# Attention's value product in plain float32, other buffer and hold-back counts, and attention traced at high priority, in a hybrid decoder layer

## Chip, cores and metric

The kernel runs on one core of a Trainium2 chip. The metric is the device time of one execution in microseconds, as the median of several runs. All arrays are float32 in the chip's main memory (DRAM).

## What is computed

One decoder layer over 2048 tokens of width 1024. An RMS norm and one input projection feed three groups of heads: differential softmax attention (4 heads, 128 wide), a gated linear recurrence (HGRN2) and a gated DeltaNet. Their outputs are concatenated, projected and added to the residual; then come a norm, a gated MLP of width 2816 with a causal convolution of width 3, and a final norm. The change touches attention:

```python
s = jnp.einsum("bhmqd,bhmkd->bhmqk", qi, kt).astype(jnp.float32) * scale
s = jnp.where(kpos[None, :] <= qpos[:, None], s, MASK_NEG)
p = jax.nn.softmax(s, axis=-1)
pd = p[:, :, 0] - lam * p[:, :, 1]
return jnp.einsum("bhqk,bhkv->bhqv", pd.astype(vt.dtype), vt)
...
o = rmsnorm(o, subln_w) * (1.0 - lambda_init)
```

and the place of the MLP's down projection in the order of the work:

```python
h = h + jnp.einsum("btf,fd->btd", jax.nn.silu(gate) * val, ffn_w_down[l])
```

## The kernel before

Large products are made of three products of type float32r: each operand is split into a high and a low part (`split`, L86), and `mm3` (L94 to L98) adds high by high, high by low and low by high. L88 (ScalarE) writes the high part and L89 (VectorE) the low one. TensorE's products of 128 rows by 512 columns on L96 to L98 are nearly all of its work; "three-term product" below means one of them. There are 9528 in the program, before and after.

Attention (`attention`, L871) goes head by head and, in a head, by blocks of 128 queries from the last block to the first. A block's keys come in chunks of 512. For each chunk and each of the two softmax maps `att_probs` makes two score products and, in the diagonal chunk, a mask product (L917, L920), a negated row maximum on VectorE (L921) and the exponential on ScalarE (L923); the two maps are then joined into one matrix on ScalarE and VectorE (L942, L943). `att_pv`, called one block later, turns each chunk over with four TensorE transposes (L954), splits it into `ph` and `pl` (L957), and multiplies both with the values, which stand in memory already split in two halves of 128 columns (L962, 256 columns each). At the block's end the two halves of the result are added (L965, L967), normed (L969 to L972), turned over (L973) and stored in `s_mix` (L976).

The keys 0 to 1023 are worked on during the input projection, with pools of their own (`XB`). Blocks 8 to 15 come later, among the MLP of the first 1024 tokens: `ffn_block` (up projection), then `down`, whose steps of 24 three-term products each load a weight tile and a tile of `s_g` (L1264 to L1270). `Pump` (L62) sets how far the attention's generator has been advanced at each MLP step; it is due by `PUMP1`. At the step (3, 8) of `down` the loop stops, attention is finished, and the output projection of tokens 1024 to 2047 runs (`residual`, L1054, called at L1027) with one `down` step drawn in after every second of its eight token tiles (L1030). `forms` (L1116) then prepares that half's operands for `up7` (L1151), a product scheme with seven products in place of eight, and a second `down` ends the kernel.

The text of the program does not set the order on an engine. The Tile framework's scheduler places the instructions on each of the five engines by readiness and by a priority that follows the order in which they were traced. Each engine then works through its own list in order.

Of the kernel before, what the change touches and what calls it, by code (L numbers as in the profile page):

```python
# [9 lines left out]
F32 = mybir.dt.float32  # L10
# [9 lines left out]
P = 128  # L20
# [6 lines left out]
EPS = 1e-6  # L27

P0_BUFS = 8
P1_BUFS = 4  # L30
S_BUFS = 2
T_BUFS = 1
XB = 6, 4, 2, 1, 2
NORM_PD = 2

# [6 lines left out]
AP_LEAD = 1  # L42

PUMP0 = 0
PUMP1 = 66
OFF = dict(aq=0, ak=512, av=1024, hq=1536, hf=1792, hi=2048, hg=2304,
           dq=2560, dk=2816, dv=3072, dz=3328, ab=3584)

# [31 lines left out]
class K:  # L80
# [66 lines left out]
    def scratch(self, ctx):  # L147
        d = ctx.enter_context(self.tc.tile_pool(name="scratch", bufs=1, space=DRAM))
        self.s_q = d.tile([4, P, 2, 2, T], F32R, name="s_q")
        self.s_k = d.tile([4, P, 2, T], F32R, name="s_k")  # L150
        self.s_v = d.tile([4, T, 2, P], F32R, name="s_v")
        self.s_dn = d.tile([8, P, T], F32, name="s_dn")
        self.s_hg = d.tile([8, P, T], F32, name="s_hg")
        self.s_mix = d.tile([8, P, T], F32, name="s_mix")
        self.s_h = d.tile([T, D], F32, name="s_h")
        self.s_g = d.tile([NF, P, T], F32, name="s_g")
# [152 lines left out]
    def proj_block(self, hf, t2, u, halo, kind, c0, i, w):  # L309
# [23 lines left out]
        if kind == "av":  # L333
            nc.scalar.copy(o, pt)
            pv = self.pp.tile([P, 512], F32, name="pp")
            for j in range(4):
                nc.tensor.transpose(pv[:, j * P:(j + 1) * P], o[:, j * P:(j + 1) * P], self.ident)
            eh, el = et("eh", F32R), et("el", F32R)
            self.split(eh, el, pv)
            for j, e in enumerate((eh, el)):  # L340
                nc.sync.dma_start(self.s_v[i, gs, j].bitcast(F32).rearrange("(k p) v -> p k v", p=P),
                                  e.bitcast(F32).rearrange("p (k v) -> p k v", v=P))
            return
        if kind == "hi":
            nc.scalar.copy(o, pt)
# [513 lines left out]

    def att_open(self, ctx, p0_bufs, p1_bufs, s_bufs, t_bufs, slots, side="left"):  # L860
        pool = partial(self.tc.tile_pool, side=side, reuse_waits="tile")
        self.p_bufs, self.kslots = (p0_bufs, p1_bufs), slots
        self.kq = ctx.enter_context(pool(name="kq", bufs=1))
        self.ap = ctx.enter_context(pool(name="ap", bufs=2))
        self.sm = ctx.enter_context(pool(name="sm", bufs=2))
        self.pss = ctx.enter_context(pool(name="pss", bufs=s_bufs, space=PSUM))
        self.pst = ctx.enter_context(pool(name="pst", bufs=t_bufs, space=PSUM))
        pso = ctx.enter_context(pool(name="pso", bufs=1, space=PSUM))
        self.oc = pso.tile([P, 2, 256], F32, name="o")

    def attention(self, b0, b1):  # L871

        nc, kq = self.nc, self.kq
        nkc = -(-b1 // 4)
        last = None
        for h in range(4):
            kS, vS = [None] * nkc, [None] * nkc
            for kc in reversed(range(nkc)):
                ts = slice(kc * 512, (kc + 1) * 512)
                slot = (h * nkc + kc) % self.kslots  # L880
                kS[kc] = kq.tile([P, 2, 512], F32R, name=f"k{slot}")
                nc.gpsimd.dma_start(kS[kc], self.s_k[h, :, :, ts])
                vS[kc] = kq.tile([P, 4, 2, P], F32R, name=f"v{slot}")
                nc.gpsimd.dma_start(vS[kc].rearrange("p k i v -> p k (i v)"),
                                    self.s_v[h, ts].rearrange("(k p) i v -> p k (i v)", p=P))
            for b in reversed(range(b0, b1)):
                if b % 2 == 1 or b == b1 - 1:
                    qS = self.ap.tile([P, 2, 2, 256], F32R, name="q")
                    q0 = b // 2 * 256
                    nc.gpsimd.dma_start(qS.rearrange("p m i q -> p (m i) q"),  # L890
                                        self.s_q[h, :, :, :, q0:q0 + 256].rearrange("p m i q -> p (m i) q"))
                pd = self.att_probs(kS, qS, b)
                if last:
                    self.att_pv(*last)
                last = h, b, pd, vS
                yield b + 1
        self.att_pv(*last)
# [47 lines left out]

    def att_pv(self, h, b, pd, vS):
        nc, sm = self.nc, self.sm
        oc = self.oc[:, b % 2]
        for c, pc in enumerate(pd):
            n = pc.shape[1]  # L950
            pt = self.pst.tile([P, 512], F32, name="t")
            for k in range(n // P):
                ks = slice(k * P, (k + 1) * P)
                nc.tensor.transpose(pt[:, ks], pc[:, ks], self.ident)  # L954
            ph = self.ap.tile([P, 512], F32R, name="ph")
            pl = self.ap.tile([P, 512], F32R, name="pl")
            self.split(ph[:, 0:n], pl[:, 0:n], pt[:, 0:n])  # L957
            for k in range(n // P):
                ks = slice(k * P, (k + 1) * P)
                vt = vS[c][:, k].rearrange("p i v -> p (i v)")  # L960
                for i, x in enumerate((ph, pl)):
                    nc.tensor.matmul(oc[:, 0:256], lhsT=x[:, ks], rhs=vt, start=c == 0 and k == 0 and i == 0,  # L962
                                     stop=c == len(pd) - 1 and ks.stop == n and i == 1)
        ol = sm.tile([P, P], F32, name="ol")
        nc.scalar.copy(ol, oc[:, P:2 * P])  # L965
        on = sm.tile([P, P], F32, name="on")
        nc.vector.tensor_tensor(on, oc[:, 0:P], ol, op=ALU.add)  # L967
        ss = sm.tile([P, 1], F32, name="ss")
        nc.scalar.activation(ol, on, AF.Square, accum_out=ss)  # L969
        rs = sm.tile([P, 1], F32, name="rs")  # L970
        self.rsqrt(rs, ss, 1.0 / P, EPS)
        nc.vector.tensor_scalar(on, on, rs, None, op0=ALU.mult)  # L972
        nc.tensor.transpose(oc[:, 0:P], on, self.ident)  # L973
        mx = sm.tile([P, P], F32, name="mx")
        nc.scalar.activation(mx, oc[:, 0:P], AF.Copy, scale=self.subln)
        nc.sync.dma_start(self.s_mix[h, :, b * P:(b + 1) * P], mx)  # L976


    def tail(self, cd, out):
# [5 lines left out]
        with ExitStack() as ctx:  # L985
# [5 lines left out]
            with ExitStack() as c1:  # L991
# [7 lines left out]
                                      lambda s, g, cs, pv: self.hi_lo(u[s][0][g][:, :, cs], u[s][1][g][:, :, cs], pv)))  # L999
                cd.close()  # L1000
                self.st = pool(c1, "cs", bufs=2)
                self.att_open(ca, P0_BUFS, P1_BUFS, S_BUFS, T_BUFS, 4, side="right")
                att = Pump(self.attention(8, 16), 4 * 100)
                pump = lambda n: att.upto((n - PUMP0) / (PUMP1 - PUMP0))
                for f in range(NF):
# [2 lines left out]
            with ExitStack() as c1:  # L1008
                self.st = pool(c1, "ds", bufs=2)
                down = self.down([0, 1], out, 1, main)  # L1010
                for s, dc, f in down:
                    n = 2 * s + dc
                    if (n, f) == (3, 8):
                        break
                    pump(2 * NF + n * NF // 2 + f // 2)
                    if (n, f) == (1, NF):
# [10 lines left out]
                for n, _ in enumerate(self.residual([2, 3], range(4), self.s_h, put, ws)):  # L1027
                    if n == 4:
                        B = next(forms)
                    if n % 2:  # L1030
                        next(down)
                for _ in chain(forms, down):
                    pass
# [329 lines left out]
```

## Time and profile before

| | |
|---|---|
| median of 3 runs | 3026.0 us (3024.95 to 3026.33) |
| the profiled execution | 3026.32 us |
| its span | 3024.6 us |
| TensorE busy (PE) | 2866.8 us, 95% |
| VectorE busy (DVE) | 1987.2 us, 66% |
| ScalarE busy (ACT) | 1393.7 us, 46% |
| GpSimd busy (POOL) | 373.5 us, 12% |
| mean granted TensorE clock | 0.975 |

Busy time is the time in which an engine has at least one instruction under way. A TensorE product's own length covers more than its share of the engine, because products overlap: the distance between the starts of two neighbours is what one of them costs. The clock is granted at 2.4 GHz or at half of that, 1.2 GHz.

### The profile page before, as it was taken

How to read it: one execution, taken by the hardware profiler on the slowest of the kernel's cores; microseconds unless marked ns; L12 is line 12 of the kernel's file. 1: busy time of each engine (PE TensorE's matmuls, PEld its weight loads, DVE VectorE, ACT ScalarE, POOL GpSimd, SP SyncE). 2: the span in 40 equal slices, each digit the busy share in tenths (PEclk: the TensorE clock that was granted, in tenths of full speed). 3: DMA queues.
4: the chain of work that ended last, by engine and by line, in shares of the span. 5: the costliest groups of instructions: out<-in, count | busy, mean ns of one | idle time of the engine just before them, and what ended most of it. 6: DMA issues, size and time to landing. Idle time of an engine off the chain costs nothing.

```text
span 3024.6 us, 50228 instructions
## 1 busy us (share of the span) xinstructions
PE 2866.8 (95%) x19746; PEld 2331.8 (77%) x19746; DVE 1987.2 (66%) x3535; ACT 1393.7 (46%) x2536; POOL 373.5 (12%) x567
## 2 busy tenths in 40 slices
PE   8899999999998899999999999999777999999998
PEld 6688877788776678887888888887555788888886
DVE  4144887578584766755677766767637788777454
ACT  3234456423222244443566666566634444444443
POOL 1001221111000102101111100001001222220000
PEclk9999999999998899999999999999888999999999
DMA  8565355243744643213423455854034222224674
GB/s 231 132 159 159 101 145 145 77 120 96 179 109 124 198 155 96 70 60 99 115 62 97 132 162 172 270 172 123 13 120 163 88 77 83 77 78 141 221 257 154
DMA packets 382928, 395.58 MB, mean 131 GB/s; under 512 B 68635, under 2 KB 280163, under 8 KB 382691
## 3 DMA queue, kind: packets, MB, share of 16 engines
q1 hardware_dynamic: 343395, 346.22, 37.4%
q0 software_dynamic: 39296, 46.14, 6.1%
q8 instruction: 155, 2.54, 0.4%
q14 instruction: 82, 0.67, 0.1%
HBM read 285.34 MB, written 106.95 MB: 130 GB/s over the span
## 4 chain that ended last, share of the span: by engine, by line
PE 87%; DVE 5%; DMA 3%; ACT 3%; issue 1%; POOL 0%; SPq 0%; POOLq 0%; ACTq 0%; DVEq 0%
PE pp L96 17%; PE pp L97 17%; PE pp L98 17%; PE pd L96 6%; PE pd L97 6%; PE pd L98 6%; PE o L962 4%; PE s L917 4%; PE t L954 2%; PE t L438 1%; PE t L804 1%; ACT p L923 1%; DMA x<-in_x_dram 1%; DMA h<-s_h 1%; DMA two<-s_mix 1%
## 5 line engine op out<-in xcount | busy, mean ns | idle before, releaser
L96 PE MATMUL pp<-uh,wh 128*128 128x512 f32 x896 | 360.6, 403 | 0.1
L97 PE MATMUL pp<-ul,wh 128*128 128x512 f32 x896 | 357.8, 399 | 0.3 <-DVE ul L191 0.3
L98 PE MATMUL pp<-uh,wl 128*128 128x512 f32 x896 | 357.1, 399 | 0.0
L89 DVE TENSOR_TENSOR wl<-two,wh 128x1024 fp32r<-128x1024 f32 x176 | 210.8, 1223 | 171.7 <-ACT wh L88 171.1
L1214 DVE SCALAR_TENSOR_TENSOR cv<-raw,columns,cv 128x512 f32<-128x512 f32 (+1 forms) x264 | 244.3, 925 | 70.3 <-ACT cv L1211 67.2
L96 PE MATMUL pd<-wh 128*128 128x512 f32 x704 | 257.8, 396 | 11.1 <-ACT wh L88 11.1
L88 ACT CAST wh<-two 128x1024 fp32r<-128x1024 f32 x176 | 178.7, 1052 | 184.4 <-PE pd L97 129.5
L921 DVE TENSOR_REDUCE nb<-s 128x1 f32<-128x512 f32 (+3 forms) x320 | 193.1, 608 | 107.2 <-PE s L920 65.0
L97 PE MATMUL pd<-wl,wh 128*128 128x512 f32 x704 | 258.3, 396 | 4.9 <-DVE wl L89 4.9
L923 ACT ACTIVATE p<-s,nb 128x512 f32<-128x512 f32 (+3 forms) x320 | 199.9, 626 | 122.2 <-DVE nb L921 105.4
L98 PE MATMUL pd<-wh,wl 128*128 128x512 f32 x704 | 248.3, 393 | 0.0
L96 PE MATMUL pp<-f,wh 128*128 128x512 f32 x616 | 241.3, 397 | 7.1 <-ACT wh L88 7.1
L97 PE MATMUL pp<-f,wh 128*128 128x512 f32 x616 | 244.5, 397 | 0.0
L98 PE MATMUL pp<-f,wl 128*128 128x512 f32 x616 | 237.1, 396 | 0.0
L917 PE MATMUL s<-k,q 128*128 128x512 f32 (+3 forms) x640 | 191.8, 390 | 25.4 <-ACT p L923 25.0
L98 PEld LDWEIGHTS pp<-uh,wl 128*128 128x128 f32 x896 | 170.2, 190 | 35.2 <-issue 0.2
L97 PEld LDWEIGHTS pp<-ul,wh 128*128 128x128 f32 x896 | 170.4, 190 | 34.5 <-DVE ul L191 1.0
L96 PEld LDWEIGHTS pp<-uh,wh 128*128 128x128 f32 x896 | 170.5, 190 | 34.1 <-ACT uh L190 0.5
L104 POOL TENSOR_TENSOR rs<-rs,mhalf 128x1 f32<-128x1 f32 x112 | 69.4, 623 | 1019.5 <-DVE rs L103 824.5
L96 PEld LDWEIGHTS pd<-wh 128*128 128x128 f32 x704 | 133.7, 190 | 40.8 <-ACT wh L88 13.2
L97 PEld LDWEIGHTS pd<-wl,wh 128*128 128x128 f32 x704 | 134.3, 191 | 33.4 <-DVE wl L89 5.4
L98 PEld LDWEIGHTS pd<-wh,wl 128*128 128x128 f32 x704 | 133.2, 189 | 28.0 <-DVE wl L89 0.2
(324 smaller groups left out, 6358.4 us busy)
## 6 DMA issues: line engine op xcount, KB each, us to landing
wu<-in_ffn_w_up_dram SPq DMA_DIRECT2D x88, 512.0 KB, 3.8
two<-in_ffn_w_down_dram SPq DMA_DIRECT2D x88, 512.0 KB, 3.8
two<-s_g SPq DMA_DIRECT2D x88, 512.0 KB, 4.7
wr<-in_w_in_dram SPq DMA_DIRECT2D x56, 512.0 KB, 4.8
q<-s_q POOLq DMA_DIRECT2D x32, 512.0 KB, 5.6
s_h<-h SPq DMA_DIRECT2D x32, 512.0 KB, 3.2
v<-s_v POOLq DMA_DIRECT2D x28, 512.0 KB, 5.4
k<-s_k POOLq DMA_DIRECT2D x28, 512.0 KB, 5.7
```

The costliest lines, as they stand in the source:

```text
L88: self.nc.scalar.copy(hi, src)
L89: self.nc.vector.tensor_tensor(lo, src, hi.bitcast(F32), op=ALU.subtract)
L96: mm(ps, lhsT=a[0], rhs=b[0], start=start, stop=False)
L97: mm(ps, lhsT=a[0], rhs=b[1], start=False, stop=False)
L98: mm(ps, lhsT=a[1], rhs=b[0], start=False, stop=stop)
L104: nc.gpsimd.tensor_tensor(out, out, self.mhalf[:, 0:1].broadcast_to(list(out.shape)), op=ALU.pow)
L917: nc.tensor.matmul(ps[:, 0:n], lhsT=qS[:, m, i, qs], rhs=kS[c][:, m, 0:n], start=i == 0, stop=i == 1 and not diag)
L921: nc.vector.tensor_reduce(nb[:, c, m:m + 1], ps[:, 0:n], axis=AX.X, op=ALU.max, negate=True)
L923: nc.scalar.activation(t, ps[:, 0:n], AF.Exp, bias=nb[:, c, m:m + 1], accum_out=ls[:, c, m:m + 1])
L954: nc.tensor.transpose(pt[:, ks], pc[:, ks], self.ident)
L962: nc.tensor.matmul(oc[:, 0:256], lhsT=x[:, ks], rhs=vt, start=c == 0 and k == 0 and i == 0, stop=c == len(pd) - 1 and ks.stop == n and i == 1)
L1214: nc.vector.scalar_tensor_tensor(c, r[e][:, j:j + n], self.fcw_l[j][:, idx:idx + 1], c, op0=mult, op1=ALU.add)
```

## The change

The probabilities and the values stay plain float32 in attention's second product: no split of the values when they are projected (L338), none of the probabilities (L957), one product of 128 columns per tile of 128 keys in place of two of 256, and no addition of halves. The block's last transpose gets a place of its own in the accumulator bank. Score buffers of the second map grow from 4 to 7, the slots for keys and values from 4 to 5 with another rule for their turn. Both halves of attention's work in a block are traced inside `high_priority()`. `PUMP1` goes from 66 to 62. The `down` loop stops at (2, 14), not (3, 8), and 13 steps, not 4, are drawn in among the eight token tiles of `residual`.

```diff
-P1_BUFS = 4
+P1_BUFS = 7
+K_SLOTS = 5
-PUMP1 = 66
+PUMP1 = 62
+HELD = 2, 14
-        self.s_v = d.tile([4, T, 2, P], F32R, name="s_v")
+        self.s_v = d.tile([4, T, P], F32, name="s_v")
-            eh, el = et("eh", F32R), et("el", F32R)
-            self.split(eh, el, pv)
-            for j, e in enumerate((eh, el)):
-                nc.sync.dma_start(self.s_v[i, gs, j].bitcast(F32).rearrange("(k p) v -> p k v", p=P),
-                                  e.bitcast(F32).rearrange("p (k v) -> p k v", v=P))
+            v = et("v")
+            nc.scalar.copy(v, pv)
+            nc.sync.dma_start(self.s_v[i, gs].rearrange("(k p) v -> p k v", p=P), v.rearrange("p (k v) -> p k v", v=P))
@@ attention
-            for kc in reversed(range(nkc)):
+            slots = [self.kfree.popleft() for _ in range(nkc)]
+            for kc, slot in enumerate(slots):
...
+            self.kfree.extend(reversed(slots))
-                pd = self.att_probs(kS, qS, b)
-                if last:
-                    self.att_pv(*last)
+                with self.tc.high_priority():
+                    pd = self.att_probs(kS, qS, b)
+                    if last:
+                        self.att_pv(*last)
@@ att_pv
-        oc = self.oc[:, b % 2]
+        oc, ot = self.oc[:, b % 2], self.oc[:, 2 + b % 2]
-            ph = self.ap.tile([P, 512], F32R, name="ph")
-            pl = self.ap.tile([P, 512], F32R, name="pl")
-            self.split(ph[:, 0:n], pl[:, 0:n], pt[:, 0:n])
+            pT = self.ap.tile([P, 512], F32, name="pT")
+            nc.scalar.copy(pT[:, 0:n], pt[:, 0:n])
             for k in range(n // P):
-                ks = slice(k * P, (k + 1) * P)
-                vt = vS[c][:, k].rearrange("p i v -> p (i v)")
-                for i, x in enumerate((ph, pl)):
-                    nc.tensor.matmul(oc[:, 0:256], lhsT=x[:, ks], rhs=vt, start=c == 0 and k == 0 and i == 0,
-                                     stop=c == len(pd) - 1 and ks.stop == n and i == 1)
-        ol = sm.tile([P, P], F32, name="ol")
-        nc.scalar.copy(ol, oc[:, P:2 * P])
-        on = sm.tile([P, P], F32, name="on")
-        nc.vector.tensor_tensor(on, oc[:, 0:P], ol, op=ALU.add)
+                nc.tensor.matmul(oc, lhsT=pT[:, k * P:(k + 1) * P], rhs=vS[c][:, k], start=c == 0 and k == 0,
+                                 stop=c == len(pd) - 1 and k == n // P - 1)
@@ tail
-                    if (n, f) == (3, 8):
+                    if (n, f) == HELD:
                         break
...
-                    if n % 2:
+                    for _ in range(13 * (n + 1) // 8 - 13 * n // 8):
                         next(down)
```

The scheduler's lists change everywhere with this. Three places follow; the names before the arrow are what an instruction writes, those behind it what it reads.

TensorE's list at the last three-term products of `down` before attention's end (`pd` is an accumulator of `down`, `s` a score, `t` a turned chunk, `o` the value product). Before:

```order
L97 MATMUL pd<-wl,wh 128x512
L98 MATMUL pd<-wh,wl 128x512
L917 MATMUL s<-k_20309,q 128x512 x2
L962 MATMUL o<-v_18197,ph 128x256
L962 MATMUL o<-v_18197,pl 128x256
```

Now:

```order
L101 MATMUL pd<-wl,wh 128x512
L102 MATMUL pd<-wh,wl 128x512
L920 MATMUL s<-k_19346,q 128x512 x2
L961 MATMUL o<-v_19352,pT 128x128 x4
L957 MATMUL t<-ident,p_20031 128x128
L920 MATMUL s<-k_19346,q 128x512 x2
L920 MATMUL s<-k_19350,q 128x256 x2
```

From these last `pd` rows on, nothing but attention stands in the list until the output projection begins. Before, that stretch holds 260 value products, 122 transposes of chunks, 108 score products and 11 block ends (L973), and it begins behind three-term product 6288. Now it holds 47 value products, 43 transposes, 20 score products and 5 block ends, and begins behind product 6096. The first score product of blocks 8 to 15 stands behind product 4323 before and 4005 now.

SyncE's list of DMA issues where the output projection of tokens 1024 to 2047 begins (`two` loads a pair of tiles, `h` a token tile of the residual). Before:

```order
L1051 DMA two<-s_mix 128x2x512 x2
L1092 DMA h<-s_h 128x1024
L1099 DMA s_h<-h 128x1024
L1092 DMA h<-s_h 128x1024
L1099 DMA s_h<-h 128x1024
L1051 DMA two<-in_ffn_w_down_dram 128x2x512
L1051 DMA two<-s_g 128x2x512
```

Now:

```order
L1048 DMA two<-s_mix 128x2x512 x2
L1089 DMA h<-s_h 128x1024
L1096 DMA s_h<-h 128x1024
L1048 DMA two<-in_ffn_w_down_dram 128x2x512
L1048 DMA two<-s_g 128x2x512
L1089 DMA h<-s_h 128x1024
L1096 DMA s_h<-h 128x1024
L1048 DMA two<-in_ffn_w_down_dram 128x2x512
L1048 DMA two<-s_g 128x2x512
L1048 DMA two<-in_ffn_w_down_dram 128x2x512
L1048 DMA two<-s_g 128x2x512
```

One or two pairs of `down` loads now stand behind every store of a token tile. From attention's end to the first product of `up7`, TensorE's list holds 336 three-term products before and 528 now; the 72 behind the last transposes of the output projection are the same in both.

TensorE's list at the end of the DeltaNet's second group of tokens, the last of its first half (`S`, `y`: state and update of the recurrence; `pp<-u`: input projection). Before:

```order
L98 MATMUL pp<-uh_6267,wl 128x512
L691 MATMUL t<-y,kd 64x64 x4
L694 MATMUL o<-y,Aq 64x64 x4
L804 MATMUL t<-QF,KS 32x16 x32
L683 MATMUL t<-S,kg 64x64 x4
L686 MATMUL t<-S,qgT 64x64 x4
```

Now:

```order
L100 MATMUL pp<-uh_5937,wh 128x512
L101 MATMUL pp<-ul_5938,wh 128x512
L693 MATMUL t<-y,kd 64x64 x4
L696 MATMUL o<-y,Aq 64x64 x4
L102 MATMUL pp<-uh_5937,wl 128x512
L100 MATMUL pp<-uh_5937,wh 128x512
```

Before, the group's last five steps stand behind product 2688, the last of the input projection, with no three-term product between them. Now the last step stands behind product 2561, with projection work on both sides.

## Rows read from the trace of the kernel before

**Rows 1.** The page: span; engine line; TensorE's busy tenths and granted clock in 40 slices.
```profile
span 3024.6 us, 50228 instructions
...
PE 2866.8 (95%) x19746; PEld 2331.8 (77%) x19746; DVE 1987.2 (66%) x3535; ACT 1393.7 (46%) x2536; POOL 373.5 (12%) x567
...
PE   8899999999998899999999999999777999999998
...
PEclk9999999999998899999999999999888999999999
```
**Rows 2.** The page: the chain that ended last, by engine.
```profile
PE 87%; DVE 5%; DMA 3%; ACT 3%; issue 1%; POOL 0%; SPq 0%; POOLq 0%; ACTq 0%; DVEq 0%
```
**Rows 3.** Stretches: length, busy PE, PEld, DVE, ACT, POOL; clock, DMA, GB/s.
```profile
1450.00:2050.00 600.00, 599.30 (x3051) 502.24 (x3050) 428.54 (x780) 373.38 (x789) 60.14 (x124) 1.00 0.46 144
2080.00:2207.00 127.00, 93.70 (x506) 71.36 (x504) 83.41 (x205) 80.45 (x224) 10.23 (x16) 0.89 0.11 27
2207.00:2345.00 138.00, 101.41 (x424) 80.49 (x424) 82.82 (x94) 55.78 (x77) 11.07 (x16) 0.86 0.46 157
```
**Rows 4.** Waits of TensorE, 2080 to 2207 us: total, times, longest.
```profile
PE s L917 <- ACT p L923: 15.9, 22, 2.5
PE o L973 <- DVE on L972: 6.1, 6, 2.4
```
**Rows 5.** Waits of TensorE, 2207 to 2345 us.
```profile
PE pd L96 <- ACT wh L88: 11.1, 5, 6.9
PE pd L96 <- ACT gh L88: 7.7, 1, 7.7
PE pp L1068 <- DVE u L1110: 5.9, 2, 5.2
```
**Rows 6.** Groups of TensorE instructions, 2080 to 2207 us: count, busy, mean ns.
```profile
L962 PE MATMUL o<-v,ph 128*128 128x256 f32 x125 | 38.8, 333 | 2.9 <-ACT ph L88 1.7 <-ACT mx L975 0.9
...
L917 PE MATMUL s<-k,q 128*128 128x512 f32 x82 | 30.3, 466 | 13.2 <-ACT p L923 13.0
L954 PE MATMUL t<-ident,p 128*128 128x128 f32 x122 | 21.1, 293 | 6.7 <-DVE pl L89 3.8 <-DVE rs L103 2.8
```
**Rows 7.** TensorE in order of time: start, length, engine, line, instruction.
```profile
2005.34 0.39 PE L97 MATMUL pd<-wl,wh 128*128 128x512 f32 x1
2005.57 0.28 PE L962 MATMUL o<-v,pl 128*128 128x256 f32 x1
2005.68 0.28 PE L962 MATMUL o<-v,ph 128*128 128x256 f32 x1
...
2247.42 1.04 PE L1068 MATMUL pp<-ident,u 128*128 128x128 f32 x8
```
**Rows 8.** The whole run's groups: the value product, and a plain float32 product.
```profile
L962 PE MATMUL o<-v,ph 128*128 128x256 f32 x544 | 146.5, 298 | 3.9 <-ACT mx L975 1.9 <-ACT ph L88 1.7
...
L583 PE MATMUL t<-gt,dn_consts 128*128 128x512 f32 x16 | 7.7, 605 | 0.0
```
**Rows 9.** TensorE in order of time, around four records of L583.
```profile
1010.45 1.88 PE L583 MATMUL t<-gt,dn_consts 128*128 128x512 f32 x4
1011.76 0.79 PE L97 MATMUL pd<-wl,gh 128*128 128x512 f32 x1
1012.39 0.39 PE L98 MATMUL pd<-wh,gl 128*128 128x512 f32 x1
```
**Rows 10.** The tile pl: VectorE's instructions, ns min/median/max.
```profile
L89 DVE TENSOR_TENSOR pl<-t,ph x160: 281/683/758, 187.2 to 2202.4; 128x512 fp32r<-128x512 f32 x112, 128x384 fp32r<-128x384 f32 x16, 128x256 fp32r<-128x256 f32 x16, 128x128 fp32r<-128x128 f32 x16
```
**Rows 11.** TensorE in order of time, at a `down` step among the output projection.
```profile
2255.37 0.80 PE L96 MATMUL pd<-wh 128*128 128x512 f32 x1 [6.91 <-ACT wh L88]
2255.96 0.63 PE L97 MATMUL pd<-wl,wh 128*128 128x512 f32 x1
2256.39 0.63 PE L96 MATMUL pd<-wh 128*128 128x512 f32 x1
```
**Rows 12.** Stretches again: the end of the input projection and what follows.
```profile
940.00:990.00 50.00, 35.69 (x703) 28.25 (x704) 32.64 (x87) 13.86 (x18) 4.91 (x3) 0.80 0.53 155
```
**Rows 13.** Waits of TensorE on attention over the whole run.
```profile
PE s L917 <- ACT p L923: 25.0, 30, 2.5
```

More of the change, by code (lines that the diff above doesn't have):

```diff
@@ L1 @@
+from collections import deque
 from contextlib import ExitStack
@@ L861, in att_open @@
         pool = partial(self.tc.tile_pool, side=side, reuse_waits="tile")
-        self.p_bufs, self.kslots = (p0_bufs, p1_bufs), slots
+        self.p_bufs, self.kfree = (p0_bufs, p1_bufs), deque(range(slots))
         self.kq = ctx.enter_context(pool(name="kq", bufs=1))
@@ L868, in att_open @@
         pso = ctx.enter_context(pool(name="pso", bufs=1, space=PSUM))
-        self.oc = pso.tile([P, 2, 256], F32, name="o")
+        self.oc = pso.tile([P, 4, P], F32, name="o")
     def attention(self, b0, b1):
@@ L876, in attention @@
         for h in range(4):
-            kS, vS = [None] * nkc, [None] * nkc
-            for kc in reversed(range(nkc)):
+            kS, vS = [], []
+            slots = [self.kfree.popleft() for _ in range(nkc)]
+            for kc, slot in enumerate(slots):
                 ts = slice(kc * 512, (kc + 1) * 512)
-                slot = (h * nkc + kc) % self.kslots
-                kS[kc] = kq.tile([P, 2, 512], F32R, name=f"k{slot}")
+                kS.append(kq.tile([P, 2, 512], F32R, name=f"k{slot}"))
                 nc.gpsimd.dma_start(kS[kc], self.s_k[h, :, :, ts])
-                vS[kc] = kq.tile([P, 4, 2, P], F32R, name=f"v{slot}")
-                nc.gpsimd.dma_start(vS[kc].rearrange("p k i v -> p k (i v)"),
-                                    self.s_v[h, ts].rearrange("(k p) i v -> p k (i v)", p=P))
+                vS.append(kq.tile([P, 4, P], F32, name=f"v{slot}"))
+                nc.gpsimd.dma_start(vS[kc], self.s_v[h, ts].rearrange("(k p) v -> p k v", p=P))
+            self.kfree.extend(reversed(slots))
             for b in reversed(range(b0, b1)):
@@ L954, in att_pv @@
                 nc.tensor.transpose(pt[:, ks], pc[:, ks], self.ident)
-            ph = self.ap.tile([P, 512], F32R, name="ph")
-            pl = self.ap.tile([P, 512], F32R, name="pl")
-            self.split(ph[:, 0:n], pl[:, 0:n], pt[:, 0:n])
+            pT = self.ap.tile([P, 512], F32, name="pT")
+            nc.scalar.copy(pT[:, 0:n], pt[:, 0:n])
             for k in range(n // P):
-                ks = slice(k * P, (k + 1) * P)
-                vt = vS[c][:, k].rearrange("p i v -> p (i v)")
-                for i, x in enumerate((ph, pl)):
-                    nc.tensor.matmul(oc[:, 0:256], lhsT=x[:, ks], rhs=vt, start=c == 0 and k == 0 and i == 0,
-                                     stop=c == len(pd) - 1 and ks.stop == n and i == 1)
-        ol = sm.tile([P, P], F32, name="ol")
-        nc.scalar.copy(ol, oc[:, P:2 * P])
-        on = sm.tile([P, P], F32, name="on")
-        nc.vector.tensor_tensor(on, oc[:, 0:P], ol, op=ALU.add)
+                nc.tensor.matmul(oc, lhsT=pT[:, k * P:(k + 1) * P], rhs=vS[c][:, k], start=c == 0 and k == 0,
+                                 stop=c == len(pd) - 1 and k == n // P - 1)
+        sq = sm.tile([P, P], F32, name="sq")
         ss = sm.tile([P, 1], F32, name="ss")
-        nc.scalar.activation(ol, on, AF.Square, accum_out=ss)
+        nc.scalar.activation(sq, oc, AF.Square, accum_out=ss)
         rs = sm.tile([P, 1], F32, name="rs")
         self.rsqrt(rs, ss, 1.0 / P, EPS)
-        nc.vector.tensor_scalar(on, on, rs, None, op0=ALU.mult)
-        nc.tensor.transpose(oc[:, 0:P], on, self.ident)
+        on = sm.tile([P, P], F32, name="on")
+        nc.vector.tensor_scalar(on, oc, rs, None, op0=ALU.mult)
+        nc.tensor.transpose(ot, on, self.ident)
         mx = sm.tile([P, P], F32, name="mx")
-        nc.scalar.activation(mx, oc[:, 0:P], AF.Copy, scale=self.subln)
+        nc.scalar.activation(mx, ot, AF.Copy, scale=self.subln)
         nc.sync.dma_start(self.s_mix[h, :, b * P:(b + 1) * P], mx)
@@ L1001, in tail @@
                 self.st = pool(c1, "cs", bufs=2)
-                self.att_open(ca, P0_BUFS, P1_BUFS, S_BUFS, T_BUFS, 4, side="right")
+                self.att_open(ca, P0_BUFS, P1_BUFS, S_BUFS, T_BUFS, K_SLOTS, side="right")
                 att = Pump(self.attention(8, 16), 4 * 100)
```

## The prediction

> **What bounds the kernel now.** The page comes first: TensorE is busy for 2866.8 of 3024.6 us, 95%, VectorE for 66% [rows 1]. The chain that ended last says the same, 87% of it on TensorE [rows 2]. So time can be saved in two ways alone: fewer columns through TensorE, or fewer holes in it. The slices show where the holes lie: a weak beginning, a dip around slices 10 and 13, and one broad dip of three slices with 7s, in which the granted clock falls as well [rows 1]. The stretch view cuts this out. From 1450 to 2050 us, with attention running beside the MLP, TensorE is busy for 599.3 of 600 us at full clock. From 2080 to 2207 us attention is alone and TensorE is busy for 93.7 of 127 us at a mean clock of 0.89. From 2207 to 2345 us the output projection runs, 101.4 of 138 us at 0.86 [rows 3]. Busy time flatters both, since an isolated product counts with its whole length. The honest measure is the distance between starts: 0.23 us for a product of 512 columns, 0.12 us for one of 256, and about 0.11 us for each of eight transposes (1.04 us less the last one's 0.27, over seven) [rows 7].
>
> By these distances the lonely stretch of attention holds: 251 value products (the 125 of `ph` and 126 of `pl`) x 0.12 = 30 us, 82 wide score products x 0.23 = 19, 122 transposes x 0.11 = 13 [rows 6], and some 5 us of smaller ones: 67 us of work in 127, so 60 us lost. What ends the waits is the chain itself: scores wait for the exponential that frees their bank, 15.9 us in 22 waits, and block ends wait for the norm, 6.1 us [rows 4]. The output projection's stretch holds 336 three-term products x 0.23 and 64 transposes x 0.11, 84 us in 138: some 54 us lost, to weight splits (11.1 us), to the first load of `s_mix` (7.7 us) and to VectorE's scaling (5.9 us) [rows 5], the rest to half clock behind each of these.
>
> **The change, term by term.** *Attention's lonely end.* By the lists it shrinks from 260 to 47 value products, 122 to 43 transposes, 108 to 20 score products and 11 to 5 block ends; the rest stands among three-term products, where nothing is lost [rows 3]. How long the rest takes has to be bounded. By score products it would be 20/108 of 127 us, 24 us; by block ends 5/11, 58 us; by value work 47 tiles of 130, 46 us. Per chunk the chain has lost VectorE's 0.68 us subtraction [rows 10], so I take 40 us. Its own work is 47 x 0.22 + 43 x 0.11 + 20 scores at about 0.2 + 1, about 20 us, so 20 are lost in place of 60: **-40 us**, with ends of 22 and 56.
>
> *The value product.* Before, 2 x 0.12 = 0.24 us per tile of 128 keys [rows 7]. The plain float32 product is not in the trace at this shape. L583 is the nearest: it is plain float32 on a full 128 x 128 weight, eight products of 512 columns in the program and 16 records [rows 8], so two passes with a weight load each. Four records from 1010.45 us on push the product after the next to 1012.39; without that one's own 0.23 they took 1.71 us, 0.43 each [rows 9]. A quarter of the columns gives 0.107 us; the transposes, which load a plain float32 weight for every 128 columns, give 0.11. So 2 x 0.11 = 0.22 per tile, 0.02 saved on 544 tiles [rows 8], **-11 us**. The ends are 0 (if a record costs 0.12 as the old ones do) and -14. The Trainium skill ("TensorE: Matmul & The Clock Gate", "Part 3: Packing small matmuls", what overlaps) states that a weight load runs beside a product only where the row groups differ. By that rule load and product add up, 2 x 0.214 us per tile, 102 us more in place of 11 less. The trace does not agree for long products: L583's records stand 0.43 us apart with a load in each [rows 9], which is little under twice the 0.23 of a float32r product of 512 columns [rows 7], so two passes and nothing for the load. At 128 columns no run here shows it; the case stays as a rival.
>
> *The output projection.* Only 4 of its tiles had a `down` step behind them; now 13 steps are spread over eight tiles. The 192 products that this moves cost what they cost before; what counts is the holes they close. The hole of 6.9 us at 2255 and the half clock behind it (six to fourteen products 0.43 apart, not 0.23; about 2.5 us) [rows 11] should go; of VectorE's 5.2 us wait [rows 5] and its half clock perhaps 6.5 us go, because 16 products now stand in front of it. The 7.7 us at the start stay: there is still nothing between the last block end and `s_mix`. The waits behind the last transposes stay too, since the same 72 products stand there. **-16 us**; ends 0 and -40.
>
> *Gated DeltaNet.* Its second group ends 127 three-term products sooner and no longer behind the input projection's last product. The stretch where it stood alone, 940 to 990 us, has TensorE busy for 35.7 of 50 us at a clock of 0.80 [rows 12]: 14 us idle, more lost. I count **-10 us**, ends 0 and -25.
>
> *High priority.* Each attention instruction is now placed as soon as the scheduler thinks it ready. Before, lagging behind, its inputs were long there. If the chip is later than the scheduler thinks, TensorE waits at the head of its list and the MLP's products wait behind it. The rows for such a wait are the 30 scores that waited 25.0 us for an exponential, 0.83 us each [rows 13]. Blocks 8 to 15 have 28 chunks in each of four heads, 112 in all. I take ten such waits, **+8 us**; ends 0 and one per chunk, +93.
>
> *Costed at nothing.* 160 subtractions of up to 0.68 us leave VectorE [rows 10], as do the additions of halves, and a copy per block leaves ScalarE: VectorE is busy for 429 and ScalarE for 373 of the 600 us in which TensorE hides them [rows 3]. If TensorE's holes closed everywhere, they would still have a quarter in hand. Values take half the bytes; slots and buffers reach further ahead; no row of TensorE's waits names a load of keys or values, so nothing on the path is bought. If the new buffers matter, it is through the scheduler's list, which is counted above.
>
> Sum: -40 - 11 - 16 - 10 + 8 = -69 us, from the profiled execution's 3026.3 us, which is 0.3 us above the median of 3026.0: **2957 us**. A measurement here can tell about 0.2% (6 us) from no change.
>
> **Rivals.**
> 1. *The held-back steps come late.* Two loads per step stand on SyncE's list behind the store of a token tile, and that waits for the tile's products and for a free buffer. If six of the 13 steps waited as the one at 2255 us did, 6.9 us each [rows 11], 41 us would come on top, or attention's end takes its long bound of 58 us and DeltaNet gives nothing: 2957 + 33 = 2990. For it: that row. Against: other `down` products now stand between.
> 2. *More closes than I count.* Attention's end at 24 us (-56), the output projection at its -40, DeltaNet at -25, no new waits: 3026 - 56 - 11 - 40 - 25 = 2894; with half of the excess, about 2925. For it: TensorE loses nothing wherever it has other products [rows 3].
> 3. *Slower: attention at the head of the list.* One wait of 0.83 us per chunk [rows 13] costs 93 us in place of 8: 2957 + 85 = 3042. It decides from (69 + 8) / 112 = 0.69 us per chunk on. For it: all scores go through two banks and wait for ScalarE whenever attention is dense. Against: waits of this kind are absent from 1450 to 2050 us [rows 3], and the MLP leaves VectorE and ScalarE a quarter of their time.
> 4. *Slower: weight loads are not hidden at 128 columns.* Load and product in turn, 0.43 us per tile in place of 0.22: 544 x 0.21 = 114 us, 3071. L583's spacing speaks against it [rows 9].
> 5. *No change.* The lists rule out that the change does nothing, but gains and waits could cancel.
>
> **How the numbers follow.** My forecast, 2935 to 2975, has a chance of 0.54, rival 1 0.17, rival 2 0.14, rival 3 0.08, rival 4 0.05 and rival 5 0.02. The range 2915 to 3003 takes in the forecast, rival 1 and most of rival 2, about 0.82. Faster is the forecast with rivals 1 and 2, 0.85; the same 0.02; slower 0.13.
>
> **What would show it.** Right: the lonely stretch of attention about 40 us long, and the one up to `up7` with fewer holes than 54 us although it holds 192 products more; value products as two records about 0.11 us apart; DeltaNet's stretch denser. Wrong: score or value products waiting 0.5 us and more, again and again, among the MLP's products; records of the value product 0.2 us apart; waits of `pd` on weight splits at each token tile. If attention's end is still above 60 us, the first term falls, and with it the forecast.

## The result and the profile after

The changed kernel takes **2953.6 us** (median of 4 runs, 2951.72 to 2957.4), the kernel before 3025.6 us beside it (4 runs, 3024.95 to 3026.33): a ratio of 0.9764, 95% interval 0.9747 to 0.9781. Forecast were 2957 us, with a range of 2915 to 3003. The profiled execution took 2955.43 us with a span of 2953.6 us, 71.0 us less than before.

The page of the changed kernel: the span, the engines, TensorE's busy tenths and granted clock in 40 slices.

```profile
span 2953.6 us, 49810 instructions
...
PE 2836.8 (96%) x19746; PEld 2314.0 (78%) x19746; DVE 1886.4 (64%) x3295; ACT 1368.5 (46%) x2472; POOL 374.9 (13%) x567
...
PE   8899998999999889999999999999797999999998
...
PEclk9999999999999899999999999999998999999999
```

Against [rows 1], TensorE's instructions are as many as before (a plain float32 product makes two records, as `ph` and `pl` did), VectorE has 240 fewer, and the broad dip of three slices has become two single 7s. The stretches of the changed kernel show what became of it; the columns are those of [rows 3].

```profile
940.00:990.00 50.00, 37.72 (x686) 30.64 (x686) 37.66 (x87) 12.16 (x15) 9.02 (x6) 0.83 0.52 149
1450.00:2050.00 600.00, 600.00 (x3178) 502.56 (x3178) 401.34 (x745) 384.60 (x845) 68.70 (x140) 1.00 0.44 135
2066.00:2099.00 33.00, 26.43 (x170) 21.48 (x168) 13.06 (x40) 18.50 (x55) 2.74 (x5) 0.95 0.03 9
2107.00:2258.00 151.00, 136.73 (x592) 110.09 (x592) 86.03 (x90) 67.08 (x88) 4.39 (x8) 0.95 0.51 171
2258.00:2301.00 43.00, 32.17 (x127) 25.46 (x127) 31.48 (x39) 15.83 (x23) 13.31 (x14) 0.84 0.35 115
```

Attention alone now fills 32 us, from 2066 to 2099, in place of 127 [rows 3]. The output projection takes 151 us with 528 three-term products, before 119 with 336 (2213.8 to 2332.8). The end of the input projection, [rows 12] before, is hardly denser: 37.7 us busy at a clock of 0.83, before 35.7 at 0.80. Counted along the traces, the 12 three-term products behind its last one (number 2688) still take 34 us, before 37, because other small products of the recurrences stand among them. The waits of TensorE in the lonely stretch, in answer to [rows 4] (total, times, longest):

```profile
PE t L957 <- ACT pT L959: 2.9, 5, 0.7
PE o L970 <- DVE on L969: 2.1, 2, 1.7
PE o L961 <- ACT mx L972: 0.9, 2, 0.5
PE s L920 <- ACT p L926: 0.6, 2, 0.4
```

The waits of scores for exponentials, 15.9 us before, are down to 0.6. In the output projection, 2099 to 2258 us, in answer to [rows 5], and behind it up to 2290 us, where `up7` begins (the last row):

```profile
PE pd L100 <- ACT wh L92: 8.6, 5, 4.3
PE pd L100 <- ACT gh L92: 7.7, 1, 7.7
PE pd L101 <- DVE wl L93: 3.0, 1, 3.0
PE pd L102 <- DVE wl L93: 1.7, 1, 1.7
PE pp L1065 <- DVE u L1107: 0.7, 1, 0.7
...
PE pp L100 <- ACT wh L92: 10.8, 1, 10.8
```

VectorE's wait (L1107) went from 5.9 us to 0.7, the first load's wait stayed at 7.7, and the weight split's wait only went from 11.1 to 8.6. The last row was 7.1 us before, so 3.7 us of this came back:

```profile
PE pp L96 <- ACT wh L88: 7.1, 1, 7.1
```

The value product: its group over the whole run (ns min/median/max).

```profile
L961 PE MATMUL o<-v,pT x1088: 270/275/582, 174.6 to 2096.7; 128*128 128x128 f32 x182
```

Fourteen of its records in a row, in order of time (start, length, instruction):

```profile
1709.77 1.72 PE L961 MATMUL o<-v,pT 128*128 128x128 f32 x14
```

A record stands 0.112 us behind the one before it ((1.72 - 0.27) / 13), a tile of 128 keys costs 0.224 us.

### The profile page after: what moved, and what is told of

It is laid out like the page before. It is cut to its first block, busy times and chain, and to the rows that moved or that the text cites. A ratio compares the mean times of both kernels' runs of the same rounds, so it can differ in the third digit from the quotient of the medians.

```text
span 2953.6 us, 49810 instructions
## 1 busy us (share of the span) xinstructions
PE 2836.8 (96%) x19746; PEld 2314.0 (78%) x19746; DVE 1886.4 (64%) x3295; ACT 1368.5 (46%) x2472; POOL 374.9 (13%) x567
## 5 line engine op out<-in xcount | busy, mean ns | idle before, releaser
L92 ACT CAST wh<-two 128x1024 fp32r<-128x1024 f32 x176 | 178.7, 1050 | 196.6 <-PE pd L101 123.3
L93 DVE TENSOR_TENSOR wl<-wr,wh 128x1024 fp32r<-128x1024 f32 x68 | 82.9, 1222 | 122.5 <-ACT wh L92 121.8
```

The source lines that it names most:

```text
L92: self.nc.scalar.copy(hi, src)
L93: self.nc.vector.tensor_tensor(lo, src, hi.bitcast(F32), op=ALU.subtract)
```

## The experiments

The question after the result was which part of the change moved attention's end. Theory A: the value product, because it takes the subtraction of `pl` from VectorE and shortens the chain from `t` to `o`, so that the scheduler finds attention's instructions ready earlier and places them among three-term products. Theory B: the high priority does it. Theory C: `PUMP1` and the held-back steps do it. Two terms of the forecast, the held steps and the price of a product, were to be measured by themselves. "Lonely stretch" means from the last three-term product of `down` to the last block end of attention. Stretches are shown as above.

### The value product alone

The kernel before with the plain float32 values and the block end of the change (the chunk loads come in the new order too); no priority, 4 score buffers, 4 slots, `PUMP1` 66, `down` held at (3, 8).

```diff
@@ against the changed kernel
-P1_BUFS = 7
+P1_BUFS = 4
-K_SLOTS = 5
+K_SLOTS = 4
-PUMP1 = 62
+PUMP1 = 66
-HELD = 2, 14
+HELD = 3, 8
...
-                with self.tc.high_priority():
-                    pd = self.att_probs(kS, qS, b)
+                pd = self.att_probs(kS, qS, b)
...
-                    for _ in range(13 * (n + 1) // 8 - 13 * n // 8):
+                    if n % 2:
```

> The kernel before with the plain float32 value product (and the new turn of the four key slots) alone: no high priority, PUMP1 66, hold at (3, 8), old buffer counts. Theory A (the value product frees VectorE and shortens the chain, so attention keeps pace by itself): attention's lonely end holds 22 value tiles in its list, so about 18 us long in place of 128, 50 us less lost, with 9 us of TensorE time and 8 us at DeltaNet: 2955 to 2970 us. Theory B (priority moves attention forward, the product saves only its own 9 to 11 us): 3010 to 3017 us.

Measured: 2966.0 us, ratio 0.9807 (0.979 to 0.9823). This part gives 59 of the 72 us. The MLP's stretch and the lonely one of this kernel:

```profile
1450.00:2050.00 600.00, 599.80 (x3187) 504.88 (x3186) 400.56 (x744) 388.47 (x846) 67.40 (x141) 1.00 0.43 137
2133.00:2147.00 14.00, 10.57 (x75) 8.54 (x73) 5.71 (x20) 8.26 (x26) 1.65 (x3) 1.00 0.03 9
```

VectorE is busy for 401 us in the first, not 429 [rows 3], and attention stands alone for 14 us. It begins earlier too, its first score of blocks 8 to 15 at 1402 us, before at 1451.

### The priority alone, and the change without it

```diff
-                pd = self.att_probs(kS, qS, b)
-                if last:
-                    self.att_pv(*last)
+                with self.tc.high_priority():
+                    pd = self.att_probs(kS, qS, b)
+                    if last:
+                        self.att_pv(*last)
```

> The kernel before with attention traced at high priority, nothing else. Theory A: little, 3010 to 3030 us, because the list still leaves 238 value products (119 tiles, not 130) to the lonely end, some 117 us. Theory B: most of the gain, 2975 to 2990 us. A third case: TensorE waits on attention among the MLP's products, over 3040 us.

> The changed kernel without high priority, all else as changed. Theory A: the lonely end holds 57 tiles, not 47, about 39 us in place of 32, and the work beside the MLP is nearly the same: 2954 to 2965 us. Theory B: attention falls behind again, over 2985 us.

Measured: in the kernel before, 3045.69 us, ratio 1.007 (1.0055 to 1.0085), 20 us slower than the 3025.1 us beside it. Taken out of the changed kernel, 2963.73 us, 0.9801 (0.9787 to 0.9816): there it is worth 10 us. Theory B falls, since alone the lonely stretch stays at 124 us:

```profile
957.00:1025.00 68.00, 52.28 (x910) 41.38 (x910) 52.41 (x111) 17.22 (x21) 13.16 (x8) 0.72 0.46 139
...
2102.00:2226.00 124.00, 90.70 (x471) 68.40 (x469) 76.34 (x189) 72.63 (x202) 9.66 (x15) 0.86 0.11 27
```

The time alone, over 3040 us, is that of the third case, but its cause isn't: over the whole run scores wait less for an exponential than before (25.0 us in 30 waits [rows 13]).

```profile
PE s L918 <- ACT p L924: 18.8, 26, 1.9
```

The first stretch above runs from the end of the input projection (product 2688) to product 2750; small products of the recurrences stand nearly alone there. It takes 68 us at a clock of 0.72, in the kernel before 50 us, but the two don't hold the same work: 910 TensorE instructions here, 459 there. What is lost shows where nearly the same work is done, at three-term product 4000, before blocks 8 to 15 begin: the priority alone is some 11 us behind the kernel before there, and loses 8 us more behind that point, 4 of them in one wait of `pd` for ScalarE's L88 between 1880 and 1990 us. In the changed kernel the priority's effect lies in front of this point too: product 4000 comes at 1366.9 us with it and at 1377.6 us without, and 8 us of that are lost from product 2688 to 2750 (45 us, and 53 without). Why the scheduler's list comes out worse in one kernel and better in the other wasn't followed further.

### Holding the steps back: alone, undone, and fewer

```diff
-                    if (n, f) == (3, 8):
+                    if (n, f) == (2, 14):
...
-                    if n % 2:
+                    for _ in range(13 * (n + 1) // 8 - 13 * n // 8):
```

The first run adds this and `PUMP1` 62 to the kernel before, the second takes it (not `PUMP1`) out of the changed kernel, the third has `HELD = 3, 2` and 8 steps.

> The kernel before with the hold at (2, 14), 13 steps in the output projection and PUMP1 62, nothing else. Theory A (the held steps close holes in the output projection but are missing beside attention): the lonely end grows from 130 to 155 tiles, about 150 us and 12 us more lost, the output projection loses some 7 to 11 us less: 3020 to 3035 us. Rival (the held steps are worth what the prediction put on them by themselves): 3005 to 3015 us.

> The changed kernel with the hold back at (3, 8) and four steps drawn in. The prediction's term says that the 13 held steps save 16 us in the output projection, but more steps now stand beside attention, whose lonely end falls from 47 to 19 tiles (5 to 8 us less lost). Held steps worth their term: 2961 to 2968 us. Held steps worth what e3 showed (nothing): 2945 to 2957 us.

> The changed kernel with 8 down steps held back instead of 14 (as many as the output projection has groups; the changed kernel has 13 to 14, the kernel before 5). Theory A (holding steps is worth nothing in either direction, since what the output projection gains is lost again at the start of the last up tile and at the end of attention): within 4 us of the changed kernel, 2950 to 2958. Rival B (a middle number has the gain of the output projection without the longer end of attention): 2940 to 2949.

Measured: alone 3027.41 us, ratio 1.0009 (1.0 to 1.0019); undone 2955.73 us, 0.976 (0.9744 to 0.9776); 8 steps 2952.49 us, 0.9755 (0.9741 to 0.977). All three are within the uncertainty of the kernel that they start from: the hold is worth nothing that can be measured, and theory C falls. (`PUMP1` was not changed by itself; the value product alone has its gain with 66.) The lonely stretch, the output projection and the beginning of `up7` where it is undone:

```profile
2128.00:2138.00 10.00, 7.31 (x55) 6.22 (x53) 0.79 (x4) 2.81 (x9) 1.10 (x2) 1.00 0.02 7
...
2146.00:2265.00 119.00, 96.63 (x401) 76.98 (x402) 67.87 (x73) 47.94 (x63) 4.39 (x8) 0.88 0.45 149
2265.00:2303.00 38.00, 31.05 (x127) 24.60 (x126) 29.97 (x36) 16.66 (x25) 14.75 (x14) 0.91 0.38 128
```

Undone, the output projection takes 119 us for 336 products; with the hold 151 us for 528. The 192 products more cost 192 x 0.227 = 44 us by themselves, so the hold closes 11 us of holes there. But `up7` begins 5 us worse with it (43 us, not 38), and the lonely stretch grows from 10 to 32 us, because the steps that are held no longer stand beside attention; 28 value tiles more move into it. Where the hold is put on the kernel before, the lonely stretch grows in the same way, to 155 us:

```profile
2018.00:2173.00 155.00, 115.49 (x639) 88.94 (x637) 106.83 (x267) 101.25 (x285) 15.78 (x24) 0.91 0.17 43
```

### VectorE's time and VectorE's place in the chain

Both runs start from the value product alone. The first gives VectorE a subtraction per chunk again, whose result nobody reads. The second puts VectorE between `t` and the product: ScalarE copies into `px`, and VectorE's maximum of `t` and `px` makes `pT`, with the same values as before.

```diff
             nc.scalar.copy(pT[:, 0:n], pt[:, 0:n])
+            px = self.ap.tile([P, 512], F32, name="px")
+            nc.vector.tensor_tensor(px[:, 0:n], pt[:, 0:n], pT[:, 0:n], op=ALU.subtract)
...
@@ the second run
-            nc.scalar.copy(pT[:, 0:n], pt[:, 0:n])
+            px = self.ap.tile([P, 512], F32, name="px")
+            nc.scalar.copy(px[:, 0:n], pt[:, 0:n])
+            nc.vector.tensor_tensor(pT[:, 0:n], pt[:, 0:n], px[:, 0:n], op=ALU.max)
```

> As e1 (value product alone, 2966.0 us), with VectorE's subtraction of the old kernel put back once per chunk into a tile that nobody reads, so that it takes VectorE's time and no place in the chain. Theory A1 (VectorE's time is what kept attention back): the list leaves 61 tiles to the lonely end, not 22, about 45 us in place of 13.6, of which some 17 us are work that moves there: 2975 to 2985 us. Theory A2 (VectorE at two thirds has time to spare, only the chain and TensorE count): 2962 to 2969 us.

> As e5, but VectorE's instruction now makes the operand that the value product reads, so it takes a place in the chain too, as the split's low part did. Theory A1 alone (time): as e5, 2975 to 2985 us. Time and chain together: the list leaves 88 tiles to the lonely end, about 75 us, 30 us of it work that moves there: 2990 to 3005 us. Neither: 2962 to 2969 us.

Measured: 2996.92 us, ratio 0.9903 (0.9886 to 0.9919), and 3015.39 us, 0.9956 (0.994 to 0.9971). So half of the 59 us goes when VectorE's instruction is back, and most of the rest when the product waits for it; both cost more than expected. Busy VectorE in the MLP's stretch, and the lonely stretch, of the first:

```profile
1450.00:2050.00 600.00, 597.72 (x3129) 502.14 (x3128) 435.00 (x801) 376.08 (x810) 69.01 (x141) 1.00 0.43 136
2130.00:2180.00 50.00, 38.46 (x236) 30.00 (x234) 35.43 (x92) 33.01 (x95) 3.31 (x6) 0.91 0.02 7
```

And of the second:

```profile
1450.00:2050.00 600.00, 600.00 (x3127) 505.65 (x3126) 429.29 (x784) 373.04 (x787) 65.38 (x137) 1.00 0.44 139
2107.00:2196.00 89.00, 63.17 (x345) 50.51 (x343) 53.06 (x128) 49.40 (x136) 5.19 (x9) 0.85 0.04 12
```

VectorE is back at 435 and 429 us (the kernel before has 429), and the lonely stretch grows from 14 to 50 and 89 us. TensorE loses at most 2.3 us of the MLP's 600 in any of them. So it isn't on the chip that VectorE holds TensorE up there: what changes is how much of attention the scheduler's list has placed by the end of it. The lists show it before anything runs: 22 value tiles in the lonely stretch with the product alone, 61 and 88 in these two, and 130 pairs in the kernel before.

Not all of the 31 and 49 us are lost there. At three-term product 4000 the first part of attention (keys 0 to 1023) is done and blocks 8 to 15 haven't begun in any of these kernels, so the traces can be cut at that product (us from the span's start to it, and from it to the end of the span):

| kernel | to product 4000 | from there on |
|---|---|---|
| before | 1372 | 1653 |
| priority alone | 1387 | 1657 |
| value product alone | 1377 | 1586 |
| the same, with the unread subtraction | 1393 | 1603 |
| the same, VectorE before the product | 1388 | 1624 |
| changed, without priority | 1378 | 1585 |
| changed | 1367 | 1587 |

The kernel before has 120 small products more left at that point than the changed one, nearly all of the DeltaNet (the priority alone 36), an estimated 6 us by the spacing in its own trace; what the value product takes off the second column is therefore 61 us. The other parts of the change take nothing off it: without priority, hold or buffers the changed kernel needs 1584 or 1585 us there. VectorE's instruction gives back 17 of the 61 us, and 38 when the product waits for it, which is what was expected of attention's end. The other 16 and 11 us are lost between products 2000 and 2750, where no attention runs; why wasn't followed. Of the 23 us that the second run leaves, 6 are TensorE's (400 tiles x 0.016); the rest, the new block end and the order of the chunks among it, wasn't taken apart.

The first run doesn't test VectorE's time by itself either. The subtraction reads `t`, of which there is one buffer (`T_BUFS = 1`), so the next chunk's transposes have to wait for it although nobody reads its result; its lonely stretch shows such a wait:

```profile
PE t L956 <- DVE px L960: 0.3, 1, 0.3
```

Whether the list comes out worse for VectorE's time or for the longer hold of `t` is open; a subtraction that reads neither `t` nor anything in the chain was not run.

### The buffers

```diff
-P1_BUFS = 7
+P1_BUFS = 4
-K_SLOTS = 5
+K_SLOTS = 4
```

> The changed kernel with 4 score buffers of the second map and 4 key and value slots in place of 7 and 5. The prediction costs them at nothing: 2950 to 2958 us; the list leaves 42 tiles to the lonely end, not 47. If the new buffers carry part of the gain: over 2960 us.

Measured: 2954.16 us, ratio 0.9757 (0.9742 to 0.9771), the changed kernel's time. The buffers are worth nothing, as costed.

### Each value product twice

```diff
+                for i in range(2):
                     nc.tensor.matmul(oc, lhsT=pT[:, k * P:(k + 1) * P], rhs=vS[c][:, k],
+                                     start=c == 0 and k == 0 and i == 0,
+                                     stop=c == len(pd) - 1 and k == n // P - 1 and i == 1)
```

> The changed kernel, but each value product is issued twice into the same sum: the attention output before its normalisation is doubled, which the normalisation takes out again up to its small constant. This adds 544 products of 128 by 128, 1088 records. Theory A (TensorE is the bound in the attention stretches, and a record costs the 0.112 us at which the records of the changed kernel follow each other, load hidden): +122 us, less what shorter waits in attention give back (the lonely end lost about 12 us): 3063 to 3076. Rival B (TensorE had idle time in attention that the second product fills, so the product term was never worth its TensorE time): under 3040. Rival C (load not hidden, about twice the price): over 3150.

Measured: 3072.43 us, ratio 1.0146 (1.013 to 1.0161), 119 us more than the changed kernel. For 1088 records that is 0.109 us each, close to the spacing of 0.112 us in the trace. This kernel's lonely stretch is 8 us long, 2205 to 2213, of which some 3 are lost in place of 12, so by this estimate 9 us of the cost came back there and a record costs between 0.109 and 0.118 us. Theory A of this run holds: a record's price is its spacing, and it goes to the time. The group of the value product:

```profile
L962 PE MATMUL o<-v,pT x2176: 270/275/377, 173.8 to 2210.9; 128*128 128x128 f32 x198
```

The MLP's stretch:

```profile
1450.00:2050.00 600.00, 600.00 (x3461) 515.25 (x3458) 359.99 (x682) 359.49 (x794) 69.52 (x144) 1.00 0.32 96
```

TensorE is busy throughout with 283 records more than in the changed kernel, and VectorE for 41 us less: everything else comes later, by as much.

### A hole near 460 us, and a version meant to beat both

Attention's first phase in the changed kernel waits for a load of keys near 460 us, as the row of TensorE's waits from 300 to 1000 us shows.

```profile
PE s L920 <- DMA k<-s_k: 3.5, 1, 3.5
```

Two stretches of the changed kernel, around that wait and behind the DeltaNet's end:

```profile
450.00:500.00 50.00, 39.80 (x586) 32.46 (x585) 42.54 (x126) 35.10 (x95) 9.59 (x14) 0.86 0.59 159
...
1050.00:1150.00 100.00, 90.78 (x614) 72.33 (x618) 69.59 (x116) 38.48 (x57) 18.59 (x20) 0.92 0.50 159
```

One more slot for that phase was to remove it; the second run has 8 held steps besides.

```diff
-XB = 6, 4, 2, 1, 2
+XB = 6, 4, 2, 1, 3
```

> The changed kernel with one more slot for the first phase (the last number of XB 3 instead of 2), so that attention's key loads there find a free slot sooner. The changed kernel waits some 7 us for a key load near 460 us, and its clock is at the lower level behind it; the first stages end 6 us later than before. Theory A (that hole costs its length and its clock): 5 to 10 us less than the changed kernel, 2943 to 2949. Rival B (the hole is made up later, since attention taken early there is work taken from later): within 3 us, 2950 to 2957.

> The one more slot and 8 held steps together, a version meant to beat both kernels. Theory A (the hole costs, the hold is worth nothing): as the run with the slot alone, 2943 to 2949. Rival B (both are worth nothing): 2950 to 2957. Rival C (both gain): 2935 to 2943.

Measured: 2966.79 us, ratio 0.9801 (0.9784 to 0.9817), and 2968.82 us, 0.9804 (0.9789 to 0.9818): 13 to 15 us slower than the changed kernel, outside every expectation. The same two stretches with the slot:

```profile
450.00:500.00 50.00, 41.42 (x636) 34.13 (x635) 46.03 (x134) 37.76 (x99) 9.97 (x13) 0.97 0.54 149
...
1050.00:1150.00 100.00, 81.50 (x545) 65.10 (x546) 64.94 (x106) 35.33 (x53) 14.29 (x16) 0.85 0.50 165
```

The wait is gone and the clock at 460 us is back at 0.97. But the hole opens again at 1050 to 1150 us, 9 us less busy and at a clock of 0.85, and the lonely stretch begins 8 us later; all 13 us are lost by three-term product 4000 (1379.5 us, changed 1366.9). So the hole was indeed made up elsewhere, as Rival B had it, and more than made up. That attention taken earlier was missing as cover there is the likeliest reading; no run separates it from other shifts of the list. No run beat the changed kernel by more than the measurement is uncertain.

## Why the prediction was right

The time was 3 us from the forecast. The terms, in spans, add up to 71 us as they did in the forecast to 69. That they meet so closely is luck: attention's end and the priority came out 8 us better each, the output projection 9 us worse, the DeltaNet 3 and the value product 2. Taken out of the kernel one by one, the parts don't follow the forecast's split either: the hold is worth nothing (forecast -16) and the priority -10 (forecast +8).

| term | forecast | found | from |
|---|---|---|---|
| attention's lonely end | -40 | -48 | 127.8 us became 32.3; of those some 20 are its own work, so 12 lost in place of 60 |
| the value product | -11 | -9 | 544 x (0.24 - 0.224) |
| output projection, held steps | -16 | -11, with +4 at `up7` | spacing of the products; as a part of the change: 0 |
| Gated DeltaNet and the rest | -10 | about -7 | the difference that is left; 5 of it between products 2688 and 2750 |
| high-priority waits | +8 | 0 | TensorE is busy for 600 of 600 us beside the MLP; as a part of the change: -10 |

*Attention's lonely end.* Right in place and mechanism: 32 us, where 40 were taken and 22 and 56 were the ends. By value work, scores and block ends the estimates had been 46, 24 and 58; the scores came nearest. What the forecast left open was why the list had changed. The runs settle which part did it: the value product alone gives 59 us, all of it behind product 4000. A VectorE instruction put back takes 17 us of that away, and 38 when the product waits for it. The step "costed at nothing" failed here. It said that the subtractions leave VectorE inside time that TensorE hides. On the chip that is so, 597.7 busy us of 600 with the subtraction back; but the same subtractions, by their time or by their place in the chain of `t`, decided where the scheduler could place attention, and that was worth more than any other part. The cost had been counted all the same, through the list, and so the sum held.

*The value product.* The records stand 0.112 us apart, between the quarter of L583's (0.107) and the old 0.12. Rival 4 falls, with the doubled product as a second witness: 0.109 us each. The rule of the Trainium skill ("TensorE: Matmul & The Clock Gate", "Part 3: Packing small matmuls", what overlaps) by which load and product would add up does not hold in this trace at 128 columns either: every one of the 1088 records has a load of its own, and none shows in the spacing.

*Gated DeltaNet.* Forecast were 10 us because the group no longer stands behind the input projection's last product. A gain of about that size is there, but it comes with the priority and not from that move: the stretch behind product 2688 is still there (34 us for 12 three-term products, before 37), filled with other small products. At product 4000 the changed kernel is 11 us ahead, the kernel before's 6 us of small products counted in, and without priority it isn't ahead at all (1377.6 us, before 1371.8 + 6).

*The output projection.* The step that failed is "what counts is the holes they close". They do close 11 us. But the held steps are the products beside which attention ran, so the holes open again in attention's end and at `up7`. Rival 1 was wrong in its place (the longest wait at a held step's weight split is 4.3 us, where six of 6.9 were feared), right in that this term could give nothing. That held steps lengthen attention's end stood nowhere in the forecast, though the list of before and now had 6288 and 6096 as the last product in front of it.

*High priority.* The forecast's +8 us, ten waits of 0.83 us, didn't come: scores waited for an exponential for 0.6 us in two waits at attention's end, and beside the MLP TensorE had no idle time. Rival 3 falls. Its sign was still possible: alone, the priority costs 20 us, some 11 of them before blocks 8 to 15 begin and none shown to come from attention's scores. Here it gains 10 us, all in front of that point. The forecast had no price for this.

*Rival 2* (more closes than counted) came halfway for attention's end, 32 us between its 24 and the forecast's 40, and not for the output projection; *rival 5* falls. Rival 1's 33 us don't follow from its own figures: its late steps give 41, its other branch 18 + 10 = 28. Two rows were read loosely, with no weight in the sum: the early dip stands in slices 13 and 14, and 0.68 us is the median of the subtractions, whose longest took 0.758.

## What to carry over

Where a scheduler orders the lists, an instruction can matter though another engine hides its time on the chip: ask of every instruction taken off or added what it lets the scheduler place earlier, and read the lists for it. Cover is a stock: steps moved into one hole are missing in another, so price both places before the gain of one is booked. And a scheduling hint has no price of its own; the same lines cost 20 us in one kernel and gave 10 in the next.

## What the chip showed that was not expected

A plain float32 product on a full 128 x 128 weight costs 0.224 us at 128 columns, two records of 0.112 us, less than the two split products of 256 columns (0.24 us) that it replaces, and it needs neither split nor addition. A transpose of the same size is a single record, at the same 0.11 us. Four times 0.112 is 0.448 us, and L583's records of 512 columns stand 0.43 us apart [rows 9]: the price grows with the columns, and nothing of the weight load that every record has is left over.
